# A second group of down chunks by Strassen's algorithm, one group amid gate and up, and a residual kept without ALPHA

## The chip, the cores and the metric

The kernel runs on one core of one Trainium2 chip. TensorE multiplies matrices, VectorE (DVE) and ScalarE (ACT) work element by element, GpSimd (POOL) and SyncE (SP) only issue transfers here. The metric is the device time of one execution in microseconds (us), from several runs, of which the median counts. Inputs lie in the chip's memory; the weights are reordered on the host before the launch, which is not timed.

## The reference

Two layers on x of 512 tokens by 1024 features, float32. Each layer is an FFN, a mixer (attention in layer 0, causal pooling in layer 1) and a second FFN, each with a residual and a layer norm, so there are six phases: FFN, attention, FFN, FFN, pooling, FFN.

```
def swiglu(x, w_gu, w_down):
    g, u = jnp.split(x @ w_gu, 2, axis=-1)        # w_gu: 1024 x 5632
    return (jax.nn.silu(g) * u) @ w_down          # w_down: 2816 x 1024

for i in range(DEPTH):                            # DEPTH = 2, ALPHA = 4 ** 0.25
    x = layer_norm(ALPHA * x + 0.5 * swiglu(x, ...), ln_g[i, 0], ln_b[i, 0])
    x = layer_norm(ALPHA * x + mixer(x), ln_g[i, 1], ln_b[i, 1])
    x = layer_norm(ALPHA * x + 0.5 * swiglu(x, ...), ln_g[i, 2], ln_b[i, 2])
```

layer_norm takes mean and variance over the 1024 features, adds 1e-5 to the variance, multiplies by g and adds b.

## The kernel before, in words

**Products.** Every float32 operand is split into a high part of reduced precision (ScalarE, L97) and the rest (VectorE, L98), and each product is three matmuls: high by low, high by high, low by high (mm3, L100 to L104). One split handles 128 partitions by 1024 elements.

**Weights.** They come as pieces of 128x1024 (512 KB). `load` (L181) issues a piece on SP into a slot of 4 KB per partition; a piece with `plus` gets a second block added by an accumulating transfer on the POOL queue (L187). `prepare` (L197) splits the next unit into a high and a low slot; raw pieces and split parts share 24 slots (SLOTS). `load_ahead` keeps up to 7 or 9 pieces loaded (RAW, and two more if `free()` allows), `run_ahead` keeps 5 parts and more prepared beyond those retired (PARTS, L208 to L212). `held` counts slots taken by other tiles.

**FFN.** The 22 chunks of 128 hidden features are handled in pairs. Pair 0 is plain; pairs 1 to 10 are quads: Strassen's algorithm with seven products (numbered 1 to 7) in place of eight, over two halves of the tokens, two halves of the input features, and gate with up. A unit of a quad is one product: two outputs, four k, three passes, 24 matmuls of 256 columns. ORDER (L150) lists the units; all x operands (seven tiles with tag "act", ACT = 7 buffers of 8 KB) live until the last quad. The result, silu(gate) times up, goes to hT for features 0 to 7 (BLOCK = 8) and to slots (`later`) for the rest.

**Down.** Features 0 to 7 go through Strassen's algorithm as well, after the last quad: seven products in the order LATER = (1, 2, 6, 5, 7, 3, 4), each with two weight tiles, two k, two token tiles and three passes, 24 matmuls of 512 columns, and each followed by two additions from PSUM into the residual ax on VectorE (L626). Their operands are made by a generator (`seven`, L295): a sum or difference where it takes one (`form`), then the split (`take`) into an "act" buffer; each `next(operands)` makes the next. The remaining 14 chunks are plain (BProduct, L418): main handles a chunk for four token tiles with 24 matmuls, and the last four chunks (five in the last phase) form a tail that goes token tile by token tile, so that the layer norm of one lies beside the matmuls of the next. Their operands are splits of pairs of chunks (`act`, L633).

**Residual.** ax holds the normalised rows of all tokens. During the phase after, VectorE turns each token tile into ALPHA times (row times g plus b), by two operations of 128x1024 (L392, L393), or one multiplication in the first FFN (L390). The rows of g and b are broadcast into tiles with tag "stage" (four buffers of 4 KB), which the feature-major copies of x use too.

**What sets the order.** TensorE runs in the order of the code. For the other engines and the queues a planner orders the instructions: at each moment of its own time model the earliest in the code among those that are ready; a tile that finds no free buffer waits for one. `tc.issue_after` puts an instruction behind another on its engine. The order is fixed at compile time, and each engine and queue then works in order. ORDER and two more places set where in the code an operand is made or a residual tile updated:

```
    ORDER = [(1, 1)] + [(i, jj + (i == 1)) for jj in QUADS for i in (2, 6, 5, 7, 3, 1, 4) if (i, jj) != (1, QUADS[-1])]
                    if 3 <= jj < 3 + NT:
                        update_residual(ins)
                if jj == QUADS[-1] and i in (2, 6, 3):
                    next(operands)
```

Of the kernel before, what the change touches and what calls it, by code (L numbers as in the profile page):

```python
# [32 lines left out]
P = 128  # L33
# [17 lines left out]
BLOCK = 8  # L51
R = 4
R_LAST = 5
SLOTS = 24
RAW = 7
PARTS = 5
ACT = 7
# [23 lines left out]
def trunk(ctx, tc, x, rel_bias, ln_g, ln_b, w_gu, w_dq, w_down, a_in, a_out, b_in, b_group, b_scale, b_out, onehot, out):  # L81
# [68 lines left out]
    ORDER = [(1, 1)] + [(i, jj + (i == 1)) for jj in QUADS for i in (2, 6, 5, 7, 3, 1, 4) if (i, jj) != (1, QUADS[-1])]  # L150

    def ffn_units(l, m):
        for i in range(4):
            plain(w_gu[l, m, 0, i])
        gu = {jj: Quad(w_gu[l, m, jj]) for jj in QUADS}
        for i, jj in ORDER:
            gu[jj].unit(i)
        both = [Quad(w_dq[l, m, q]) for q in range(2)]
        pieces[-10:] = [q.pieces[i] for group in ((0,), (1,), (2,), (3,), (4,)) for q in both for i in group]
        for i in LATER:  # L160
            for q in both:
                q.unit(i)
        b_plain(w_down[l, m], range(BLOCK, NF))

# [14 lines left out]
    parts, taken, retired, held = [], [0], [0], [0]  # L179
# [63 lines left out]
    class Plain:  # L243

        def __init__(self, name):
            self.name, self.st, self.parts = name, {}, {}

        def stage(self, half, h):
            if (half, h) not in self.st:
                self.st[half, h] = lnp.tile([P, 4, 256], F32, tag="stage", bufs=4, name=f"st{self.name}_{half}_{h}")  # L250
            return self.st[half, h]
# [14 lines left out]
    class Seven(Plain):  # L266
# [20 lines left out]
        def sums(self):  # L287

            b11, b21, b12, b22 = (self.st[i] for i in ((0, 0), (1, 0), (0, 1), (1, 1)))
# [5 lines left out]
        def seven(self, b11, b21, b12, b22, room):  # L295
# [7 lines left out]
            self.form(6, u2, b11, -1.0, b22, ALU.subtract)  # L303
            self.take(5, b11)
# [27 lines left out]

    def ln_params(n):
        l, i = lns[n]
        gt = lnp.tile([P, D], F32, tag="stage", bufs=4, name=f"lng{n}")
        bt = lnp.tile([P, D], F32, tag="stage", bufs=4, name=f"lnb{n}")
        nc.sync.dma_start(gt, ln_g[l, i:i + 1, :].to_broadcast([P, D]))
        nc.sync.dma_start(bt, ln_b[l, i:i + 1, :].to_broadcast([P, D]))
        return gt, bt

    class LayerNorm:
        def __init__(self, n, t, scale):
            self.n, self.t, self.scale = n, t, scale
# [8 lines left out]
        def normalize(self, gt, bt):  # L352
# [4 lines left out]
            nc.vector.tensor_scalar(ve, var, EPS, None, op0=ALU.add)  # L357
# [19 lines left out]
    row = [None, None]  # L377

    def load_residual():
        if residual[0][1] is not None:  # L380
            row[:] = ln_params(residual[0][1])
# [120 lines left out]
    def ffn(n, x, dest):  # L502
        with tc.tile_pool(name=f"ffn{n}", bufs=1) as fp:
            hT = fp.tile([P, BLOCK, S], F32, name=f"hT{n}")
            later, kept = {}, {}

            def features(f):

                return hT[:, f, :] if f < BLOCK else later[f // 2][:, f % 2, :]

            def room(jj):

                if 2 * jj >= BLOCK:
# [32 lines left out]
            for h, xi in enumerate(((1, 2), (8, 3))):  # L546
# [12 lines left out]
                if h == 0:  # L559
                    x.sums()  # L560

            hid = Seven(f"h{n}")
            hv = hT.rearrange("p (j c) s -> p j c s", c=2)
            operands = hid.seven(*(hv[:, 0:BLOCK // 2, c, h * 256:(h + 1) * 256] for h in range(2) for c in range(2)),
                                 lambda: fp.tile([P, 4, 256], F32, tag="ca", name=f"u2{n}"))

            quads = {}
            for i, jj in ORDER:
                if n == 0 and (i, jj) == (1, 2):
                    columns()  # L570
                    onehots = bias_load()
# [31 lines left out]
                if jj == QUADS[-1] and i in (2, 6, 3):  # L603
                    next(operands)

            accs = {0: (bank(0, f"da{n}_0"), bank(1, f"da{n}_1"))}
            for i in LATER:
                if i in (2, 5):  # L610
                    g = BANKS[i]
                    accs[g] = [bank(2 * g + t, f"d{n}_{i}_{t}") for t in range(2)]
                acc = accs[BANKS[i]]
                for q in range(2):
                    wh, wl = weights()
                    for k in range(2):
                        c = slice(k * 512, (k + 1) * 512)
                        for t in range(2):
                            o = hid.parts[i][:, :, 2 * q + k, t * P:(t + 1) * P]
                            mm3(acc[t], o[:, 0], o[:, 1], wh[:, c], wl[:, c], q == 0 and k == 0 and i in (1, 2, 5),  # L620
# [292 lines left out]
```

## Time and profile before

| | |
|---|---|
| median of 3 runs | 1727.77 us (1726.58 to 1728.12) |
| the profiled execution | 1726.37 us |
| its span, first to last instruction | 1724.2 us |
| granted TensorE clock over the span | 0.999 of full speed (2.4 GHz) |
| bytes moved by transfers | 257.30 MB, 149 GB/s on average |

The profile shows one execution. Busy time is the time in which an engine works on an instruction; matmuls overlap each other, so the time from one start to the next is shorter than one matmul's duration. PE is TensorE's matmuls, PEld its weight loads beside them. L98 is line 98 of the kernel. A wait is the idle time of an engine before an instruction, with what ended it.

### The profile page before, as it was taken

How to read it: one execution, taken by the hardware profiler on the slowest of the kernel's cores; microseconds unless marked ns; L12 is line 12 of the kernel's file. 1: busy time of each engine (PE TensorE's matmuls, PEld its weight loads, DVE VectorE, ACT ScalarE, POOL GpSimd, SP SyncE). 2: the span in 40 equal slices, each digit the busy share in tenths (PEclk: the TensorE clock that was granted, in tenths of full speed). 3: DMA queues.
4: the chain of work that ended last, by engine and by line, in shares of the span. 5: the costliest groups of instructions: out<-in, count | busy, mean ns of one | idle time of the engine just before them, and what ended most of it. 6: DMA issues, size and time to landing. Idle time of an engine off the chain costs nothing.

```text
span 1724.2 us, 27993 instructions
## 1 busy us (share of the span) xinstructions
PE 1701.4 (99%) x11555; PEld 1582.5 (92%) x11555; DVE 1240.8 (72%) x1657; ACT 824.8 (48%) x1161; POOL 93.8 (5%) x132
## 2 busy tenths in 40 slices
PE   8999999999999999999999999999999999999998
PEld 8999998898888899999888999998898899999886
DVE  6876697365666977778929777789279887777945
ACT  6544455164444554445525544455244464455620
POOL 1120000000000000000000000000000000000000
PEclk9999999999999999999999999999999999999999
DMA  9776566232224376655743766657322556665611
GB/s 306 194 233 176 141 175 218 78 99 86 85 81 129 77 203 172 172 149 142 238 123 76 204 173 170 149 144 235 98 74 98 145 173 176 171 172 153 183 51 49
DMA packets 84863, 257.30 MB, mean 149 GB/s; under 512 B 8128, under 2 KB 25576, under 8 KB 84736
## 3 DMA queue, kind: packets, MB, share of 16 engines
q1 hardware_dynamic: 70080, 202.40, 35.6%
q0 software_dynamic: 14656, 53.12, 17.9%
q8 instruction: 90, 1.47, 0.4%
q14 instruction: 37, 0.30, 0.1%
HBM read 253.37 MB, written 4.74 MB: 150 GB/s over the span
## 4 chain that ended last, share of the span: by engine, by line
PE 94%; DVE 4%; DMA 1%; issue 1%; ACT 0%; SPq 0%; DVEq 0%; POOLq 0%
PE gu L102 17%; PE gu L103 17%; PE gu L104 17%; PE acc L102 7%; PE acc L104 7%; PE acc L103 7%; PE qk L102 2%; PE qk L103 2%; PE qk L104 2%; PE da L102 2%; PE da L103 2%; PE da L104 2%; PE d L102 1%; PE d L103 1%; PE d L104 1%; DVE lo L98 1%
## 5 line engine op out<-in xcount | busy, mean ns | idle before, releaser
L102 PE MATMUL gu<-x,hi 128*128 128x256 f32 x2496 | 708.7, 284 | 5.3 <-DVE x L98 5.3
L98 DVE TENSOR_TENSOR lo<-raw,hi 128x1024 fp32r<-128x1024 f32 x458 | 555.8, 1221 | 211.3 <-PE acc L102 92.5
L103 PE MATMUL gu<-x,hi 128*128 128x256 f32 x2496 | 706.8, 283 | 0.0
L104 PE MATMUL gu<-x,lo 128*128 128x256 f32 x2496 | 706.8, 283 | 0.0
L97 ACT ACTIVATE hi<-raw 128x1024 fp32r<-128x1024 f32 x458 | 479.2, 1056 | 369.0 <-DVE lo L98 252.4
L102 PEld LDWEIGHTS gu<-x,hi 128*128 128x128 f32 x2496 | 479.7, 192 | 8.3 <-DVE x L98 7.1
L103 PEld LDWEIGHTS gu<-x,hi 128*128 128x128 f32 x2496 | 479.7, 192 | 0.0
L104 PEld LDWEIGHTS gu<-x,lo 128*128 128x128 f32 x2496 | 479.6, 192 | 0.0
L102 PE MATMUL acc<-lo,h 128*128 128x512 f32 x448 | 174.8, 390 | 0.0
L104 PE MATMUL acc<-hi,h 128*128 128x512 f32 x448 | 174.3, 389 | 0.0
L103 PE MATMUL acc<-hi,h 128*128 128x512 f32 x448 | 174.3, 389 | 0.0
L187 POOL DMA_DIRECT2D raw<-in_ffn_w_gu x80 | 68.7, 859 | 1061.6 <-DMA raw<-in_ffn_w_gu 606.9
L140 DVE TENSOR_TENSOR raw<-raw,raw 128x1024 f32<-128x1024 f32 x96 | 117.1, 1220 | 8.6 <-DMA raw<-in_ffn_w_dq 7.2
L522 ACT ACTIVATE kept<-gu 128x512 f32<-128x512 f32 x120 | 71.1, 592 | 98.5 <-PE gu L104 98.5
L104 PEld LDWEIGHTS acc<-hi,h 128*128 128x128 f32 x448 | 84.1, 188 | 17.6
L103 PEld LDWEIGHTS acc<-hi,h 128*128 128x128 f32 x448 | 84.1, 188 | 17.2
L102 PEld LDWEIGHTS acc<-lo,h 128*128 128x128 f32 x448 | 84.1, 188 | 17.1
L525 DVE TENSOR_TENSOR cb<-gu,kept 128x512 f32<-128x512 f32 x40 | 27.6, 689 | 67.7 <-PE gu L104 67.7
L349 DVE SCALAR_TENSOR_TENSOR ax<-acc,ax 128x512 f32<-128x512 f32 x48 | 33.0, 688 | 55.7 <-PE acc L104 55.3
L328 ACT ACTIVATE st<-tp,cols 128x128 f32<-128x128 f32 x140 | 53.5, 468 | 23.7 <-PE tp L317 23.7
L529 ACT ACTIVATE sg<-cb 128x256 f32<-128x256 f32 x40 | 16.5, 412 | 94.5 <-DVE cb L525 94.5
L98 DVE TENSOR_TENSOR x<-st,x 128x512 fp32r<-128x512 f32 (+1 forms) x64 | 51.4, 820 | 12.2 <-ACT x L97 12.2
(155 smaller groups left out, 2193.5 us busy)
## 6 DMA issues: line engine op xcount, KB each, us to landing
raw<-in_ffn_w_gu SPq DMA_DIRECT2D x216, 512.0 KB, 4.6
raw<-in_ffn_w_gu POOLq DMA_DIRECT2D x80, 512.0 KB, 6.3
raw<-in_ffn_w_down SPq DMA_DIRECT2D x56, 512.0 KB, 4.3
raw<-in_ffn_w_dq SPq DMA_DIRECT2D x40, 512.0 KB, 3.6
raw<-in_a_w_in SPq DMA_DIRECT2D x24, 512.0 KB, 3.9
raw<-in_ffn_w_dq POOLq DMA_DIRECT2D x16, 512.0 KB, 6.8
raw<-in_a_w_out SPq DMA_DIRECT2D x8, 512.0 KB, 3.6
raw<-in_b_w_in SPq DMA_DIRECT2D x8, 512.0 KB, 5.2
```

The lines of the kernel that those rows point to most:

```text
L97: nc.scalar.activation(hi, src, AF.Copy)
L98: return nc.vector.tensor_tensor(lo, src, hi.bitcast(F32), op=ALU.subtract)
L102: nc.tensor.matmul(acc, sh, ml, start=first, stop=False, skip_group_check=shared)
L103: nc.tensor.matmul(acc, sh, mh, start=False, stop=False, skip_group_check=shared)
L104: nc.tensor.matmul(acc, sl, mh, start=False, stop=last, skip_group_check=shared)
L140: nc.vector.tensor_tensor(d, d, more, op=ALU.add)
L187: nc.gpsimd.dma_start(p.tile, p.plus, accum_op=ALU.add)
L328: nc.scalar.activation(src[:, i, :], tp[:, c], AF.Identity, scale=g, bias=b)
L349: nc.vector.scalar_tensor_tensor(r, y, self.scale, r, op0=ALU.mult, op1=ALU.add)
L522: nc.scalar.activation(kept[i, jj], acc, AF.Copy)
L525: nc.vector.tensor_tensor(out, two(acc), two(kept.pop((i, jj))), op=ALU.add)
L529: nc.scalar.activation(sg, g, AF.Silu, scale=sign)
```

## The change

Sixteen of the 22 down chunks go through Strassen's algorithm, in two groups of eight. The products of the first group stand in ORDER at quad 7 (MIDDLE): the first of them before that quad's unit 4, the other six behind it. Those of the second group follow the last quad. Six chunks stay plain. There are nine "act" buffers and 20 slots; the four "stage" buffers become one of 16 KB, which holds the second group's features too, and the norms' rows go to slots. The operand of a product is made after the weights of later ones in the code (`retire`, then `next(operands)`), and in the first group one call each at units 6 and 7 of quad 7 and after products 1, 2, 6, 5 and 7. ax is kept without ALPHA: its sums are divided by ALPHA and the norm's epsilon by ALPHA squared. Its g is multiplied in by one VectorE operation, its b added by an accumulating broadcast transfer on the POOL queue; the first FFN's rows need neither. Pooling's pT goes to "act" buffers.

```diff
-SLOTS = 24
+SLOTS = 20
+GROUP = 8
-BLOCK = 8
+BLOCK = 16
-ACT = 7
+ACT = 9
+MIDDLE = 7
...
+    ORDER = [(1, 1)]
+    for jj in QUADS:
+        after = [] if jj == QUADS[-1] else [(1, jj + 1)]
+        seven = [(i, jj) for i in (2, 6, 5, 7, 3, 4)]
+        if jj == MIDDLE:
+            group = [(i, FF) for i in LATER]
+            ORDER += seven[:-1] + group[:1] + seven[-1:] + group[1:] + after
+        else:
+            ORDER += seven[:-1] + after + seven[-1:]
+    ORDER += [(i, FF + g) for g in range(1, BLOCK // GROUP) for i in LATER]
...
     def free():
-        return SLOTS - RAW - 2 * PARTS - held[0]
+        return SLOTS - RAW - 2 * PARTS - sum(held)
 
     def load_ahead():
-        while len(loaded) < len(pieces) and sum(p.uses > 0 for p in loaded[-32:]) < RAW + 2 * (free() > 1):
+        while len(loaded) < len(pieces) and sum(p.uses > 0 for p in loaded[-32:]) < RAW + 2 * (free() > 1) + min(0, free()):
             load()
...
             self.form(6, u2, b11, -1.0, b22, ALU.subtract)
+            yield
             self.take(5, b11)
...
     def update_residual(after, count=1):
 
-        with tc.issue_after(after.ins):
-            for _ in range(count):
-                t, n = residual.pop(0)
-                gt, bt = row
-                if n is None:
-                    nc.vector.tensor_scalar(ax[:, t, :], ax[:, t, :], ALPHA, None, op0=ALU.mult)
-                else:
-                    nc.vector.scalar_tensor_tensor(ax[:, t, :], ax[:, t, :], ALPHA, gt, op0=ALU.mult, op1=ALU.mult)
-                    nc.vector.scalar_tensor_tensor(ax[:, t, :], bt, ALPHA, ax[:, t, :], op0=ALU.mult, op1=ALU.add)
+        for _ in range(min(count, len(residual))):
+            t, n = residual.pop(0)
+            with tc.issue_after(after.ins):
+                nc.vector.tensor_tensor(ax[:, t, :], ax[:, t, :], row[0], op=ALU.mult)
+            nc.gpsimd.dma_start(ax[:, t, :], ln_row(ln_b, n), accum_op=ALU.add)
+            if not residual:
+                held[1] = 0
...
+            hid = [Seven(f"h{n}_{g}") for g in range(BLOCK // GROUP)]
+
+            def form():
+
+                for g, h in enumerate(hid):
+                    hv = hT[g].rearrange("p (j c) s -> p j c s", c=2)
+                    yield from h.seven(*(hv[:, :, c, t * 256:(t + 1) * 256] for t in range(2) for c in range(2)),
+                                       lambda: fp.tile([P, 4, 256], F32, tag="ca", name=f"u2{n}_{g}"))
+
+            operands = form()
+            accs = {}
+
+            def down_product(i, g):
+
+
+                if i in (1, 2, 5):
+                    b0 = {1: (2, 6), 2: (0, 2), 5: (4, 4)}[i][g]
+                    accs[g, BANKS[i]] = [bank(b0 + t, f"d{n}_{g}_{i}_{t}") for t in range(2)]
+                acc = accs[g, BANKS[i]]
+                for q in range(2):
+                    wh, wl = weights()
+                    for k in range(2):
+                        c = slice(k * 512, (k + 1) * 512)
+                        for t in range(2):
+                            o = hid[g].parts[i][:, :, 2 * q + k, t * P:(t + 1) * P]
+                            mm3(acc[t], o[:, 0], o[:, 1], wh[:, c], wl[:, c], q == 0 and k == 0 and i in (1, 2, 5),
+                                q == 1 and k == 1 and i in (2, 3, 4), True)
+                for t0, d, sign in {1: ((0, 0, 1),), 2: ((0, 0, 1),), 6: ((2, 0, 1),), 5: ((2, 1, -1),), 7: ((2, 1, -1),),
+                                    3: ((2, 0, 1),), 4: ((0, 1, -1),)}[i]:
+                    for t in range(2):
+                        r = ax[:, t0 + t, d * 512:(d + 1) * 512]
+                        nc.vector.scalar_tensor_tensor(r, acc[t], 0.5 / ALPHA * sign, r, op0=ALU.mult, op1=ALU.add)
+                retire(2)
+                if i in ((1, 2, 6, 5, 7) if g == 0 else (1, 2, 6, 5)):
+                    next(operands)
...
-                if jj == QUADS[-1] and i in (2, 6, 3):
+                if (i, jj) in ((6, MIDDLE), (7, MIDDLE), (2, QUADS[-1]), (6, QUADS[-1]), (3, QUADS[-1])):
                     next(operands)
...
-            down.main((3, 1, 2, 0))
+            down.main((1, 0, 2, 3))
...
     def pooling(n, x, dest):
-        held[0] = 6
+        held[0] = 0
...
-                    pT[g] = [wp.tile([P, 2, S], F32R, tag="slot", bufs=SLOTS, name=f"pT{i}_{g}") for i in range(2)]
+                    pT[g] = glob.tile([P, 2, 2, S], F32R, tag="act", bufs=ACT, name=f"pT{g}")
```

## Rows read from the trace of the kernel before

**Rows 1.** The page: busy time by engine, and the chain that ended last.

```profile
...
PE 1701.4 (99%) x11555; PEld 1582.5 (92%) x11555; DVE 1240.8 (72%) x1657; ACT 824.8 (48%) x1161; POOL 93.8 (5%) x132
...
PE 94%; DVE 4%; DMA 1%; issue 1%; ACT 0%; SPq 0%; DVEq 0%; POOLq 0%
...
```

**Rows 2.** Who made TensorE wait (us in total, times, longest).

```profile
...
PE gu L102 <- DVE x L98: 5.3, 6, 1.0
...
```

**Rows 3.** Busy time by stage: seven down products, plain down, a quad.

```profile
...
core 0: us, PE busy (x) PEld busy (x) DVE busy (x) ACT busy (x) POOL busy (x), PEclk, DMA share, GB/s
239.30:277.40 38.10, 38.10 (x171) 31.54 (x170) 38.10 (x42) 26.70 (x28) 1.20 (x3) 1.00 0.70 218
277.40:331.90 54.50, 54.50 (x242) 45.16 (x241) 21.26 (x20) 13.68 (x13) 0.00 (x0) 1.00 0.44 137
1440.30:1460.50 20.20, 20.20 (x170) 20.20 (x170) 13.89 (x16) 10.29 (x14) 1.71 (x2) 1.00 0.71 183
...
```

**Rows 4.** Groups by line and shape: busy us, mean ns | idle before.

```profile
...
L98 DVE TENSOR_TENSOR lo<-raw,hi 128x1024 fp32r<-128x1024 f32 x458 | 555.8, 1221 | 211.3 <-PE acc L102 92.5 <-ACT hi L97 71.6 <-PE gu L103 27.0
...
L97 ACT ACTIVATE hi<-raw 128x1024 fp32r<-128x1024 f32 x458 | 479.2, 1056 | 369.0 <-DVE lo L98 252.4 <-PE gu L103 50.1 <-issue 28.4
...
L140 DVE TENSOR_TENSOR raw<-raw,raw 128x1024 f32<-128x1024 f32 x96 | 117.1, 1220 | 8.6 <-DMA raw<-in_ffn_w_dq 7.2
...
L102 PE MATMUL da<-lo,xh 128*128 128x512 f32 x128 | 49.8, 389 | 0.0
...
L393 DVE SCALAR_TENSOR_TENSOR ax<-lnb,ax 128x1024 f32<-128x1024 f32 x20 | 24.1, 1219 | 0.0
...
L626 DVE SCALAR_TENSOR_TENSOR ax<-da,ax 128x512 f32<-128x512 f32 x32 | 20.5, 684 | 0.0
...
L187 POOL DMA_DIRECT2D raw<-in_ffn_w_dq x16 | 13.7, 854 | 170.4 <-DMA raw<-in_ffn_w_dq 72.0 <-DVE lo L98 67.3 <-DVE hT L530 22.8
...
```

**Rows 5.** TensorE in order of time: start us, duration, instruction.

```profile
...
236.30 0.39 PE L102 MATMUL gu<-x,hi 128*128 128x256 f32 x1
...
239.28 0.40 PE L102 MATMUL da<-lo,xh 128*128 128x512 f32 x1
...
252.91 0.39 PE L102 MATMUL da<-lo,xh 128*128 128x512 f32 x1
...
255.63 0.39 PE L102 MATMUL d<-lo,xh 128*128 128x512 f32 x1
...
```

**Rows 6.** VectorE in order of time, about those starts.

```profile
...
238.82 0.68 DVE L525 TENSOR_TENSOR ca<-gu,kept 128x512 f32<-128x512 f32 x1
...
252.90 1.28 DVE L626 SCALAR_TENSOR_TENSOR ax<-d,ax 128x512 f32<-128x512 f32 x2
254.10 1.22 DVE L98 TENSOR_TENSOR xh<-hT,xh 128x1024 fp32r<-128x1024 f32 x1
255.23 2.35 DVE L98 TENSOR_TENSOR lo<-raw,hi 128x1024 fp32r<-128x1024 f32 x2
257.50 1.28 DVE L626 SCALAR_TENSOR_TENSOR ax<-da,ax 128x512 f32<-128x512 f32 x2
...
```

**Rows 7.** VectorE in order of time, before and in the first FFN's tail.

```profile
...
331.59 1.23 DVE L98 TENSOR_TENSOR lo<-raw,hi 128x1024 fp32r<-128x1024 f32 x1 [4.22 <-PE acc L102]
...
353.52 1.22 DVE L98 TENSOR_TENSOR lo<-raw,hi 128x1024 fp32r<-128x1024 f32 x1
...
356.77 1.23 DVE L98 TENSOR_TENSOR lo<-raw,hi 128x1024 fp32r<-128x1024 f32 x1
...
```

**Rows 8.** TensorE in order of time, where attention starts.

```profile
...
356.31 0.39 PE L102 MATMUL qk<-x,hi 128*128 128x256 f32 x1 [0.80 <-DVE x L98]
...
```

**Rows 9.** DMA issues: KB each, median us to landing.

```profile
...
raw<-in_ffn_w_dq SPq DMA_DIRECT2D x40, 512.0 KB, 3.6
...
raw<-in_ffn_w_dq POOLq DMA_DIRECT2D x16, 512.0 KB, 6.8
...
```

**Rows 10.** Who made VectorE wait for weight transfers.

```profile
...
DVE raw L140 <- DMA raw<-in_ffn_w_dq: 7.2, 6, 2.0
...
```

More of the change, by code (lines that the diff above doesn't have):

```diff
@@ L154, in ffn_units @@
             plain(w_gu[l, m, 0, i])
-        gu = {jj: Quad(w_gu[l, m, jj]) for jj in QUADS}
+        made = {}
         for i, jj in ORDER:
[L157 to L162, printed above, removed]
+            if jj < FF:
+                if i == 1:
+                    made[jj] = Quad(w_gu[l, m, jj])
+                made[jj].unit(i)
+            else:
+                if i == 1:
+                    both = [Quad(w_dq[l, m, 2 * (jj - FF) + q]) for q in range(2)]
+                    pieces[-10:] = [q.pieces[k] for k in range(5) for q in both]
+                for q in both:
+                    q.unit(i)
         b_plain(w_down[l, m], range(BLOCK, NF))
@@ L177, in trunk @@
     ffn_units(1, 1)
-    parts, taken, retired, held = [], [0], [0], [0]
+    parts, taken, retired, held = [], [0], [0], [0, 0]
     def load():
@@ L245, in __init__ @@
         def __init__(self, name):
-            self.name, self.st, self.parts = name, {}, {}
+            self.name, self.st, self.parts = name, None, {}
         def stage(self, half, h):
-            if (half, h) not in self.st:
-                self.st[half, h] = lnp.tile([P, 4, 256], F32, tag="stage", bufs=4, name=f"st{self.name}_{half}_{h}")
-            return self.st[half, h]
+            if self.st is None:
+                self.st = lnp.tile([P, 4, 4, 256], F32, tag="stage", name=f"st{self.name}")
+            return self.st[:, 2 * half + h]
         def parts_of(self, half):
@@ L287, in sums @@
         def sums(self):
-            b11, b21, b12, b22 = (self.st[i] for i in ((0, 0), (1, 0), (0, 1), (1, 1)))
+            b11, b21, b12, b22 = (self.stage(*i) for i in ((0, 0), (1, 0), (0, 1), (1, 1)))
             self.form(5, b11, b11, 1.0, b12, ALU.subtract)
@@ L329, in to_feature_major, with ln_row @@
         dest.put(t, half, src)
+    def ln_row(w, n):
+        l, i = lns[n]
+        return w[l, i:i + 1, :].to_broadcast([P, D])
     def ln_params(n):
[L334 to L339, printed above, removed]
+        rows = []
+        for nm, w in (("g", ln_g), ("b", ln_b)):
+            rows.append(wp.tile([P, D], F32, tag="slot", bufs=SLOTS, name=f"ln{nm}{n}"))
+            nc.sync.dma_start(rows[-1], ln_row(w, n))
+        return rows
     class LayerNorm:
         def __init__(self, n, t, scale):
-            self.n, self.t, self.scale = n, t, scale
+            self.n, self.t, self.scale = n, t, scale / ALPHA
             self.st = lnp.tile([P, 12], F32, tag="st", bufs=2, name=f"st{n}_{t}")
@@ L560, in ffn @@
                     x.sums()
[L562 to L565, printed above, removed]
+            hid = [Seven(f"h{n}_{g}") for g in range(BLOCK // GROUP)]
[27 more added lines that the diff above has]
+                    next(operands)
             quads = {}
             for i, jj in ORDER:
+                if jj >= FF:
+                    down_product(i, jj - FF)
+                    continue
                 if n == 0 and (i, jj) == (1, 2):
@@ L872, in trunk @@
     late.append(lambda: [to_feature_major(xs[0], 3, half, ax[:, 3, :]) for half in range(2)] + [run_ahead()])
-    residual.extend((t, None) for t in range(NT))
     for i, phase in enumerate((ffn, attention, ffn, ffn, pooling, ffn)):
```

48 lines of the change are left out of this document (15 added, 33 removed).

## The prediction

> **What bounds the kernel now.** I read the page's shares and chain first, then who makes TensorE wait, then the stages by time. TensorE is busy for 1701.4 of 1724.2 us, and the chain that ends last lies on it for 94% [rows 1]. It waits almost for nothing: the largest wait inside the work is 5.3 us in six pieces, at the starts of phases, for a layer-normed input [rows 2]. So time is TensorE's own work, and a matmul less is time less, as long as VectorE keeps its operands coming. That is the second thing to see: in the 38.1 us of the seven down products VectorE is busy for all 38.1 us, in a quad of gate and up for 13.89 of 20.20, in the plain down stage for 21.26 of 54.50 [rows 3]. VectorE is full in one stage only, and the change doubles that stage.
>
> **What goes from TensorE.** Eight plain chunks are 8 x 4 x 2 x 3 = 192 matmuls of 128x512; by seven products of two weight tiles, two k, two t and three passes they are 168. 24 go per FFN, 96 in all. A matmul's busy time of 389 ns [rows 4] is not its price, since they overlap; the pitch is. From 252.91 to 255.63 twelve start, 0.2267 us each [rows 5], and the whole stage says the same: 38.10/168 = 0.2268 [rows 3]. 96 x 0.2267 = **21.8 us**.
> The Trainium skill (TensorE: Matmul & The Clock Gate, Back-to-back issue gap) gives about 131 ns as the sustained spacing of 512-column matmuls. By it the 96 would be worth an estimated 12.6 us. The trace's stage of the same matmuls disagrees, with 226.7 ns, and the measurement decides.
>
> **What comes to VectorE and ScalarE.** Per FFN: 14 weight splits in place of 8 (+6), 4 weight sums, 7 operand splits in place of 4 pairs (+3), 4 operand sums, and 14 additions into ax. A 128x1024 operation takes 1.22 us alone and 1.135 us in a row, a pair of additions 1.20 us (250.63, 252.90, 254.10) [rows 4, 6]. That is 17 x 1.135 + 14 x 0.60 = 27.7 us per FFN, 111 us in all. The second residual operation goes: 20 x 1.14 = 23 us [rows 4] (the first FFN's four multiplies go too, uncounted). VectorE ends near 1240.8 + 111 - 23 = 1329 us of some 1705, ScalarE gains 9 x 1.06 x 4 = 38 us on 825 [rows 1, 4]. Neither becomes the bound over the whole; the question is local.
>
> **The middle group (products amid quad 7).** Its VectorE work is 29 operations x 1.135 + 14 x 0.60 = 41.3 us, beside 38.1 us of products and 2.88 us of the one gate/up unit among them (24 x 0.12 us, 236.30 to 239.28 with the next start [rows 5]). So it is as full as the stage before was, and that one starved nothing, because its operands were split far ahead. Here they can't be: the quad's x still holds seven of nine operand buffers, so two remain, and the operand of a product can be split only when the product two before it has ended. Behind that end VectorE has, in the order that the code issues: the two additions (1.20), one weight split whose slots come free at the same moment (1.14; the other's come half a product earlier), then the operand's split (1.22, ScalarE's 1.06 beside the first two). Before, additions began late: TensorE left a product at 255.63, the addition began at 257.50, 1.87 us on, for VectorE was in two weight splits [rows 5, 6]. 1.87 + 1.20 + 1.14 + 1.22 = 5.43 us against the 5.44 us of the product between. Nothing is left over, and nothing much is lost. Bounds: zero, if VectorE comes to the additions at once (3.6 of 5.44 us; the quads before leave it 6.3 us free each [rows 3], in which sums can go ahead); 4.5 us per FFN, if both weight splits stand in front (6.56, 1.12 too much, for the four operands of products 5, 7, 3 and 4). I take 1.0 us per FFN, nearer to the zero end, as a late operand gives VectorE the same time to catch up: **+4.0 us**. Product 6 has the gate/up unit as extra cover.
>
> **The group at the end.** Seven products as before, x's buffers coming free under them, fewer plain splits beside them. One thing is new: the first product writes bank 6, which the last quad's unit 3 used. That unit ended at 236.30, VectorE read its bank from 238.82 to 239.50, and the first product would start at 239.28 [rows 5, 6]. 0.2 us late, with a semaphore 0.3; bounds 0 and 1.2 us (one split more in front of it). 4 x 0.3 = **+1.2 us**. Behind it two plain chunks and four tail ones (six instead of fourteen, 32.6 us) hold three pairs of operand splits instead of seven; VectorE has 33 us idle there now [rows 3], so this cover may shrink.
>
> **Twenty slots instead of 24.** Working parts and raw pieces claim them all, before as after: the last split before the tail waited 4.22 us for TensorE to give a slot back [rows 7]. In the tail four parts are held to its end. Before, the tail's planning went six parts past the retired chunks, now five, so that one or two parts fewer of the next phase lie ready. The next ones were split at 353.52 and 356.77 [rows 7]. An FFN asks for its second part 2.88 us after its start, its third 5.76: covered. Attention and pooling ask for the third part 1.44 us after theirs, 356.31 + 1.44 = 357.75 [rows 8], and one place later it is ready at 356.77 + 1.23 = 358.0. I take 0.5 us for each of those two, **+1.0 us**, bounds 0 and 3.2 us (the spacing of the two splits).
>
> **At nothing.** Loads: six more 512 KB transfers per FFN, about 12.6 MB on 257, in stages that move 140 to 220 GB/s [rows 3]; a piece lands 3.6 us after its issue, an accumulated one 6.8 [rows 9], and nine pieces (in the last group seven) are loaded ahead. The bias transfers: twenty accumulations on the POOL queue, 0.85 us of issue each, with POOL busy 1.71 us of a quad [rows 3, 4]; behind each waits the next weight accumulation of that queue, and behind that VectorE's weight sum, which waited 7.2 us in six times for such transfers without TensorE noticing [rows 2, 10]. If that cover is gone a transfer costs up to 6.8 us; I take 0, since the pieces are loaded several units ahead. The bias lands a quad or more before ax is next read. The normalisation's constants change no instruction; its rows now come through slots, on SP, with nothing urgent behind them. The order of tiles in the plain stage follows the banks that come free; 4.1 us separate the last product from its banks' reuse, as before.
>
> **Sum.** The profiled execution took 1726.37 us (span 1724.2 and 2.2 around it), 1.4 under the median 1727.77. 1726.4 - 21.8 + 4.0 + 1.2 + 1.0 = 1710.8; on the median's footing **1712 us**.
>
> **Rivals.**
> - The operand waits eat the gain. Weight splits are issued ahead of the operand, so both may stand before it: 1.12 us for each of four operands, 17.9 us in all, 1727.8 - 21.8 + 17.9 + 2.2 = 1726, no change. For it: the order of the code, and the lag of 1.87 us. Against: half a product of earlier slots for one of the splits.
> - Slower: the same queue with the operand's own sum in it. The place is the middle group, products 7 and 4, whose operand needs a sum, then ScalarE's copy, then the split. If none of it is done ahead: 1.87 + 1.20 + 2.27 + 1.14 + 1.06 + 1.22 = 8.8 us against 5.44, 3.3 us each, with 1.12 for products 5 and 3: 8.9 us per FFN, 1727.8 - 21.8 + 35.6 + 2.2 = 1744. It decides from 1.2 us per operand on (19.6 us over sixteen). For it: VectorE full for 41 us. Against: the sums read features that are ready since quad 3, and the quads before have room for them.
> - Each removed matmul is worth less than its pitch. The nearest row for a lower price is the 256-column matmul's 0.12 us [rows 5]: 96 x 0.12 = 11.5 us, less 6.2 of waits, so 1722. For it: weight loads take 1582.5 us of TensorE's span beside the matmuls [rows 1]. Against: the whole stage runs at 0.2268. The Trainium skill's spacing, named above, would put it near this rival.
>
> **Chances.** The forecast 0.68, its own range 1705 to 1719. No change by operand waits 0.15 (a third of it still faster). Slower by the sums 0.11. Cheaper matmuls 0.06. A measurement of this kernel tells 0.2%, 3.5 us, from no change. Faster 0.68 + 0.06 + 0.05 = 0.79; same 0.08; slower the rest, 0.13. The lower end is the full 21.8 us with no wait (1706) and a run's spread; the upper end, 1727, takes in the cheap matmuls and the eaten gain, and leaves the slower case out.
>
> **What would show it.** TensorE with 96 matmuls of 128x512 fewer and the same pitch of 0.227 us in both groups; its waits for VectorE's operand copies (xh) near 1 us per FFN, all in the middle group; VectorE near 1329 us. Gaps of more than 1.2 us before products 5, 7, 3 and 4 would be the slower rival, waits on the bank at the first product of the last group the small one, a wait for weight parts at the starts of attention and pooling the slots. It is wrong if TensorE's idle time grows by more than 10 us, or if it starves at a place not named here.

## The result, and the profile after

The median fell from 1727.17 us (six runs, 1726.13 to 1728.12) to **1713.65 us** (six runs, 1711.82 to 1715.64), a ratio of 0.9922 with a 95% interval of 0.9909 to 0.9934: 13.5 us faster, where 15.8 were forecast. The profiled execution took 1713.76 us, its span is 1712.0 us, 12.2 less than before. So it came out as forecast in sign and size, but two errors of opposite sign stand in the working: the size is in part luck, and one of the errors is the lesson of this case.

The page, busy time by engine and the chain that ended last, as [rows 1]:

```profile
...
PE 1684.5 (98%) x11459; PEld 1564.8 (91%) x11459; DVE 1328.1 (78%) x1757; ACT 860.1 (50%) x1197; POOL 125.7 (7%) x168
...
PE 87%; DVE 7%; DMA 4%; issue 1%; ACT 1%; SPq 0%; DVEq 0%; POOLq 0%; ACTq 0%
...
```

VectorE has 1328.1 us, as worked out (1329), ScalarE 860.1 (863). The 96 matmuls are gone (11555 to 11459). But TensorE's share of the chain fell from 94% to 87%, and DMA has 4% of it now. Who made TensorE wait (us in total, times, longest), as [rows 2]:

```profile
...
PE d L104 <- ACT xh L99: 4.0, 3, 2.1
PE gu L104 <- DVE x L100: 3.4, 6, 0.8
PE d L106 <- DVE xh L100: 2.3, 3, 0.8
...
```

There is a new wait, 6.3 us for operands of the down products (xh), in three places of two pieces each. The old wait for x has shrunk from 5.3 to 3.4 us. A wait is not all that is lost: taking each start of a matmul less the one before, and from that the undisturbed pitch (0.2267 us for 512 columns, 0.12 for 256), the sum over the whole trace, transposes left out, is 15.4 us before and 25.2 us after, so 9.8 of the 21.8 us came back as loss. I call this sum lost time below. It lies in the middle groups of three FFNs: 0.04 us in the first, 4.8, 3.0 and 2.4 in the others, 10.1 in these three. Such a figure comes from the one execution that was profiled. In this trace and in those of five versions below that leave these three groups alike, or try a cure that does not work, one group lost 2.2 to 5.0 us and the three 9.1 to 12.1 in all; a difference of a microsecond or two between such runs shows no effect. The windows of these four groups, in order (busy time of each engine, clock, DMA share, GB/s), as [rows 3]:

```profile
...
core 0: us, PE busy (x) PEld busy (x) DVE busy (x) ACT busy (x) POOL busy (x), PEclk, DMA share, GB/s
175.60:216.60 41.00, 41.00 (x194) 34.42 (x193) 39.07 (x43) 22.23 (x23) 3.45 (x4) 1.00 0.74 199
738.90:784.70 45.80, 42.93 (x195) 35.29 (x194) 43.67 (x47) 24.00 (x26) 3.46 (x4) 0.96 0.77 194
1082.40:1126.30 43.90, 41.82 (x194) 34.16 (x193) 41.69 (x46) 23.33 (x25) 3.45 (x4) 1.00 0.76 199
1528.40:1571.80 43.40, 42.00 (x195) 34.28 (x194) 41.18 (x45) 23.31 (x25) 3.45 (x4) 1.00 0.79 204
...
```

The first FFN's group has no idle TensorE in 41.0 us. The second's lasts 45.8. What the first FFN lacks, beside everything that they share, is a residual with g and b: no row is loaded, nothing multiplied, no bias transferred.

Inside the second one. TensorE, in order of time (start, duration), as [rows 5]:

```profile
...
755.00 0.50 PE L104 MATMUL d<-lo,xh 128*128 128x512 f32 x1 [2.09 <-ACT xh L99]
...
756.50 0.79 PE L106 MATMUL d<-hi,xh 128*128 128x512 f32 x1 [0.77 <-DVE xh L100]
757.10 0.63 PE L104 MATMUL d<-lo,xh 128*128 128x512 f32 x1
757.52 0.63 PE L105 MATMUL d<-hi,xh 128*128 128x512 f32 x1
...
```

The matmul at 755.00 is the first of product 6, and it waited 2.09 us for ScalarE's part of its operand and then 0.77 for VectorE's. VectorE, as [rows 6]:

```profile
...
732.19 1.23 DVE L142 TENSOR_TENSOR raw<-raw,raw 128x1024 f32<-128x1024 f32 x1 [2.79 <-DMA raw<-in_ffn_w_dq]
...
738.79 1.22 DVE L142 TENSOR_TENSOR raw<-raw,raw 128x1024 f32<-128x1024 f32 x1 [4.24 <-DMA raw<-in_ffn_w_dq]
...
752.55 1.22 DVE L300 SCALAR_TENSOR_TENSOR u<-hT 128x1024 f32<-128x1024 f32 x1
...
755.23 1.22 DVE L100 TENSOR_TENSOR xh<-u,xh 128x1024 fp32r<-128x1024 f32 x1
...
```

It stood at two weight sums (L142) for 2.79 and 4.24 us, because the pieces that they add had not landed. It works in order, so everything planned behind them came later by that: 13.8 us after the start of the second of them the difference for operand 6 (u), and behind that its split (755.23). By TensorE's time product 6 was due at 752.7. And the POOL queue, where those pieces are accumulated:

```profile
...
722.59 0.86 POOL L203 DMA_DIRECT2D raw<-in_ffn_w_dq  x1 [18.63 <-DMA raw<-in_ffn_w_dq]
723.26 1.08 POOL L412 DMA_DIRECT2D ax<-in_ln_b  x1
725.46 0.86 POOL L203 DMA_DIRECT2D raw<-in_ffn_w_dq  x1 [1.11 <-ACT sg L552]
...
```

Between the weight accumulations of 722.59 and 725.46 stands the bias transfer of quad 6. The issues of that stretch (716 to 745 us; KB, median us to landing), as [rows 9]:

```profile
...
raw<-in_ffn_w_dq SPq DMA_DIRECT2D x6, 512.0 KB, 6.0
raw<-in_ffn_w_dq POOLq DMA_DIRECT2D x4, 512.0 KB, 9.5
ax<-in_ln_b POOLq DMA_DIRECT2D x1, 512.0 KB, 12.7
...
```

The weight accumulations took 9.5 us there, the bias transfer 12.7. Over the whole run VectorE's sums waited 31.6 us for such pieces, 18.5 of it at the first two sums for these three groups; 7.2 before [rows 10]:

```profile
...
L104 PE MATMUL d<-lo,xh 128*128 128x512 f32 x448 | 175.8, 392 | 4.4 <-ACT xh L99 4.0
...
L142 DVE TENSOR_TENSOR raw<-raw,raw 128x1024 f32<-128x1024 f32 x112 | 136.8, 1221 | 33.4 <-DMA raw<-in_ffn_w_dq 31.6
...
```

### The profile page after: what moved, and what is told of

The parts are those of the page before. It is cut to its first block, busy times and chain, and to the rows that moved or that the text cites. A ratio compares the mean times of both kernels' runs of the same rounds, so it can differ in the third digit from the quotient of the medians.

```text
span 1712.0 us, 28171 instructions
## 1 busy us (share of the span) xinstructions
PE 1684.5 (98%) x11459; PEld 1564.8 (91%) x11459; DVE 1328.1 (78%) x1757; ACT 860.1 (50%) x1197; POOL 125.7 (7%) x168
## 2 busy tenths in 40 slices
DMA packets 90482, 277.77 MB, mean 162 GB/s; under 512 B 8752, under 2 KB 26200, under 8 KB 90352
## 4 chain that ended last, share of the span: by engine, by line
PE 87%; DVE 7%; DMA 4%; issue 1%; ACT 1%; SPq 0%; DVEq 0%; POOLq 0%; ACTq 0%
PE gu L104 16%; PE gu L106 15%; PE gu L105 15%; PE d L106 5%; PE d L104 5%; PE d L105 5%; PE acc L106 4%; PE acc L105 4%; PE acc L104 4%; DMA raw<-in_ffn_w_dq 4%; DVE lo L100 2%; PE qk L104 2%; PE qk L106 2%; PE qk L105 2%; PE tp L334 1%
## 5 line engine op out<-in xcount | busy, mean ns | idle before, releaser
L99 ACT ACTIVATE hi<-raw 128x1024 fp32r<-128x1024 f32 x482 | 505.8, 1058 | 449.2 <-DVE lo L100 182.5
L100 DVE TENSOR_TENSOR lo<-raw,hi 128x1024 fp32r<-128x1024 f32 x482 | 585.1, 1219 | 154.4 <-ACT hi L99 133.9
L104 PE MATMUL d<-lo,xh 128*128 128x512 f32 x448 | 175.8, 392 | 4.4 <-ACT xh L99 4.0
L106 PE MATMUL d<-hi,xh 128*128 128x512 f32 x448 | 175.6, 392 | 2.3 <-DVE xh L100 2.3
L105 PE MATMUL d<-hi,xh 128*128 128x512 f32 x448 | 175.0, 391 | 0.0
L142 DVE TENSOR_TENSOR raw<-raw,raw 128x1024 f32<-128x1024 f32 x112 | 136.8, 1221 | 33.4 <-DMA raw<-in_ffn_w_dq 31.6
L104 PEld LDWEIGHTS d<-lo,xh 128*128 128x128 f32 x448 | 84.5, 189 | 23.1 <-ACT xh L99 5.3
L106 PEld LDWEIGHTS d<-hi,xh 128*128 128x128 f32 x448 | 84.5, 189 | 22.1 <-DVE xh L100 4.5
L105 PEld LDWEIGHTS d<-hi,xh 128*128 128x128 f32 x448 | 84.5, 189 | 17.1
L545 ACT ACTIVATE kept<-gu 128x512 f32<-128x512 f32 x120 | 70.5, 587 | 55.6 <-PE gu L106 55.4
L104 PE MATMUL acc<-lo,h 128*128 128x512 f32 x192 | 75.3, 392 | 0.0
L106 PE MATMUL acc<-hi,h 128*128 128x512 f32 x192 | 74.8, 389 | 0.0
L105 PE MATMUL acc<-hi,h 128*128 128x512 f32 x192 | 74.8, 389 | 0.0
L616 DVE SCALAR_TENSOR_TENSOR ax<-d,ax 128x512 f32<-128x512 f32 x112 | 72.4, 681 | 1.6 <-PE d L106 1.5
```

The lines of the kernel that those rows point to most:

```text
L99: nc.scalar.activation(hi, src, AF.Copy)
L100: return nc.vector.tensor_tensor(lo, src, hi.bitcast(F32), op=ALU.subtract)
L104: nc.tensor.matmul(acc, sh, ml, start=first, stop=False, skip_group_check=shared)
L105: nc.tensor.matmul(acc, sh, mh, start=False, stop=False, skip_group_check=shared)
L106: nc.tensor.matmul(acc, sl, mh, start=False, stop=last, skip_group_check=shared)
L142: nc.vector.tensor_tensor(d, d, more, op=ALU.add)
```

## The experiments

**Theory T**, formed on these rows: a bias transfer that stands in the POOL queue ahead of a weight accumulation of the middle group makes it land late; VectorE, in order, stands at the weight sum; the difference for operand 6, planned behind it, is late, and TensorE waits. **Rival A**, the forecast's own: VectorE is too full, with two operand buffers and the weights ahead of the operand. **Rival B**: the slot that the g row holds until quad 6 makes the group's loads late. What an experiment does to the middle groups is given as lost time of the four FFNs, after the change 0.04, 4.8, 3.0, 2.4.

**No bias transfer.**

```diff
                 nc.vector.tensor_tensor(ax[:, t, :], ax[:, t, :], row[0], op=ALU.mult)
-            nc.gpsimd.dma_start(ax[:, t, :], ln_row(ln_b, n), accum_op=ALU.add)
```

> Leaves out the twenty accumulating transfers of the bias row (so b is missing from the residual); VectorE's multiplication by g and the slot of the g row stay. Theory T (the transfer behind quad 6 stands in the POOL queue and on the DMA rings between the weight accumulations of the middle group, VectorE stands in order at a weight sum until they land, and the difference for operand 6 comes late): the waits of TensorE in the middle groups, 10.1 us over three FFNs, fall to under 2 us, 1704 to 1706 us. Rival A (VectorE is simply too full with two operand buffers): VectorE has the same work, the waits stay at 8 us or more, 1712 to 1714. Rival B (the slot that the g row holds until quad 6 makes the loads of the group late): the waits stay for the most part, 6 to 10 us.

1706.0 us (ratio to the kernel before 0.9879, 0.9864 to 0.9894), lost time 0.04, 0.5, 0.05, 0.7. T holds, A falls: VectorE does the same work and TensorE hardly waits. The same stretch of the second FFN, POOL and its landings, then VectorE:

```profile
...
722.60 0.86 POOL L203 DMA_DIRECT2D raw<-in_ffn_w_dq  x1 [24.40 <-DMA raw<-in_ffn_w_dq]
725.46 0.86 POOL L203 DMA_DIRECT2D raw<-in_ffn_w_dq  x1 [2.00 <-DMA raw<-in_ffn_w_dq]
...
```

```profile
...
raw<-in_ffn_w_dq SPq DMA_DIRECT2D x6, 512.0 KB, 4.8
raw<-in_ffn_w_dq POOLq DMA_DIRECT2D x4, 512.0 KB, 7.9
...
```

```profile
...
731.52 1.23 DVE L142 TENSOR_TENSOR raw<-raw,raw 128x1024 f32<-128x1024 f32 x1 [1.99 <-DMA raw<-in_ffn_w_dq]
...
735.59 1.22 DVE L142 TENSOR_TENSOR raw<-raw,raw 128x1024 f32<-128x1024 f32 x1 [1.71 <-DMA raw<-in_ffn_w_dq]
...
749.35 1.22 DVE L300 SCALAR_TENSOR_TENSOR u<-hT 128x1024 f32<-128x1024 f32 x1
...
```

The second accumulation was issued at the same moment, 725.46, but the sum that needs it began at 735.59, not 738.79. So the bias transfer costs no time on the issuing queue; it costs 3.2 us on the way. The Trainium skill (DMA: Bandwidth & Descriptors, Issuing engines are not separate DMA queues) says that transfers from all engines share the same 16 DMA engines, and that more issuing engines save no more than issue time. The pair of runs agrees with the first half: beside the bias transfer the pieces issued on SP land later too, in a median of 6.0 us, not 4.8. No run here issues the bias transfer from another engine. The 3.2 us are no accident of this FFN: in the traces of the changed kernel and all its versions below, the second accumulation of a middle group took 11.6 to 13.3 us to land where a bias transfer stands just ahead of it (19 places) and 7.8 to 10.0 where none does.

**The update a quad earlier.**

```diff
-                    if 3 <= jj < 3 + NT:
+                    if 2 <= jj < 2 + NT:
```

> The residual's update of an FFN behind quads 2 to 5 instead of 3 to 6: same work, a quad further from the middle group, and the slot of the g row free a quad earlier. T and rival B alike: waits in the middle groups under 2 us, 1704 to 1706 us, a version faster than both. Rival A: quad 6 gives VectorE 1.1 us more room, no more: the waits stay at 7 us or more, 1711 to 1713.

1704.85 us (0.9873, 0.9856 to 0.9889); lost time 0.04 us in each of the four groups. With one number changed 8.8 us come back (8.4 when each version is held against the kernel before in its own runs). Its POOL queue, the landing in the same window (716 to 745 us), and VectorE:

```profile
...
720.08 0.86 POOL L203 DMA_DIRECT2D raw<-in_ffn_w_dq  x1 [16.26 <-DMA raw<-in_ffn_w_dq]
722.85 0.86 POOL L203 DMA_DIRECT2D raw<-in_ffn_w_dq  x1 [1.91 <-DMA raw<-in_ffn_w_dq]
...
```

```profile
...
raw<-in_ffn_w_dq POOLq DMA_DIRECT2D x4, 512.0 KB, 6.4
...
```

```profile
...
729.29 1.21 DVE L142 TENSOR_TENSOR raw<-raw,raw 128x1024 f32<-128x1024 f32 x1
...
731.68 1.22 DVE L142 TENSOR_TENSOR raw<-raw,raw 128x1024 f32<-128x1024 f32 x1
...
746.32 1.22 DVE L300 SCALAR_TENSOR_TENSOR u<-hT 128x1024 f32<-128x1024 f32 x1
...
749.01 1.22 DVE L100 TENSOR_TENSOR xh<-u,xh 128x1024 fp32r<-128x1024 f32 x1
...
```

The second accumulation is issued 2.6 us earlier than in the two runs above (722.85), and the accumulations land in a median of 6.4 us; VectorE waits for neither sum, and the difference is made at 746.32, 6.2 us earlier than after the change: 3.2 us are the transfer's (752.55 to 749.35 in the run without it), 3.0 the earlier issue's. The earlier issue goes with the g row's slot, which is free a quad sooner: wherever that slot is held until quad 6 the second accumulation is issued 12.8 to 13.6 us ahead of the group, with or without transfers, and wherever it is not, 14.2 to 15.9, also in the first FFN of the run below that multiplies at quad 6 there and holds no row. Rival B is thus part of it: in the run without transfers, which holds the slot, 1.1 us more is lost over the three FFNs (0.5 and 0.7 us in two of them), here nothing.

**The operand ahead of the weights in the code.**

```diff
-                retire(2)
                 if i in ((1, 2, 6, 5, 7) if g == 0 else (1, 2, 6, 5)):
                     next(operands)
+                retire(2)
```

> In the down products the next operand is made ahead of the next weights in the code, not behind them. T: what is late is the difference for operand 6 behind the weight sums, so putting it ahead takes some of the wait away, 2 to 6 us of the 10.1, but VectorE still stands at a weight sum for 3 to 4 us in three FFNs. Rival A: the order of two weight splits and an operand was the cause, the waits fall to under 1 us, about 1704.

1713.61 us in one run; lost time 0.04, 2.2, 2.9, 4.2: 9.4 in all against 10.2, no more than such runs differ by. Rival A's cure does not cure, and T's estimate of some relief missed too. In the second FFN the difference does come sooner behind the late sum, 12.6 us instead of 13.8, but a sum for a later operand now stands ahead of its split, which comes 16.0 us behind the late sum instead of 16.4.

**Transfers added to the first FFN.**

```diff
                         update_residual(ins)
+                        if n == 0:
+                            nc.gpsimd.dma_start(ax[:, jj - 3, :], ln_row(ln_b, 0), accum_op=ALU.add)
```

> Adds four accumulating transfers of a bias row to the first FFN too, behind quads 3 to 6 (its residual is then wrong by those rows); no VectorE work and no g row is added there. That FFN has no wait in its middle group now (0.04 us). T: it gets one of 1.5 to 5 us, as the others have, 1715 to 1718 us. Rivals A and B: it stays under 0.5 us, 1713 to 1714.

1716.21 us, but not for the reason expected: the first FFN's middle group lost 0.04 us. With nothing on VectorE to hold them back the transfers were issued at the start of the phase (9.3 to 21.5 us), far from quads 3 to 6, and TensorE lost 2.2 us at 41 us, in a wait that the trace puts down to ScalarE's copy of a unit's result (L545); what made that late was not followed up. A test of a place has to make sure of the place.

**Only quad 6's transfer left out.**

```diff
...
-            nc.gpsimd.dma_start(ax[:, t, :], ln_row(ln_b, n), accum_op=ALU.add)
+            if bias:
+                nc.gpsimd.dma_start(ax[:, t, :], ln_row(ln_b, n), accum_op=ALU.add)
...
-                        update_residual(ins)
+                        update_residual(ins, bias=jj < 6)
```

> Leaves out only the bias transfer behind quad 6 in each FFN (four of twenty; b is then missing from one token tile); those behind quads 3 to 5 stay. T: this one alone stands among the weight accumulations of the middle group, so the waits of TensorE there fall from 10.1 us to what the run without any transfer has left, 1 to 2 us, 1705 to 1707 us. If transfers load the DMA rings over a longer stretch, the waits stay at 4 us or more.

1705.83 us in one run, lost time 0.04, 0.4, 0.6, 0.4: what the run without any transfer has. Twenty transfers are five phases of four, and the first FFN has none, so three stand at quad 6 of an FFN (the expectation counted four). The other seventeen cost nothing that these runs show; without the three beside the group's accumulations 8.8 of the 10.1 us are gone.

**The bias on VectorE.**

```diff
...
-            row[0] = wp.tile([P, D], F32, tag="slot", bufs=SLOTS, name=f"lng{n}")
-            nc.sync.dma_start(row[0], ln_row(ln_g, n))
-            held[1] = 1
+            row[:] = ln_params(residual[0][1])
+            held[1] = 2
...
                 nc.vector.tensor_tensor(ax[:, t, :], ax[:, t, :], row[0], op=ALU.mult)
-            nc.gpsimd.dma_start(ax[:, t, :], ln_row(ln_b, n), accum_op=ALU.add)
+                nc.vector.tensor_tensor(ax[:, t, :], ax[:, t, :], row[1], op=ALU.add)
...
-                    if 3 <= jj < 3 + NT:
+                    if 2 <= jj < 2 + NT:
```

> The bias added by VectorE from a second row slot, no bias transfers, updates behind quads 2 to 5: 1.14 us more of VectorE in each of twenty places, 23 us in all, and one slot less while the rows are held. T: no transfer stands in the way, VectorE has 6 us free in these quads, so within 2 us of the version with transfers a quad earlier, 1704 to 1707. Rival A (VectorE too full): 3 us slower or more, 1708 and up.

1705.31 us (0.9873, 0.9856 to 0.9889), lost time 0.04 in each group. 21 us more of VectorE by the profiles' pages (1349.5, against 1328.8 in the run with the update a quad earlier) change nothing: A falls a second time, and the bias by transfers gains nothing over the old way of adding it, once it stands where it does no harm.

**The first FFN again, gated.** Its tiles are multiplied by 1 on VectorE behind unit 3 of quads 3 to 6, with and without the transfer behind that:

```diff
                         update_residual(ins)
+                        if n == 0:
+                            with tc.issue_after(ins.ins):
+                                nc.vector.tensor_scalar(ax[:, jj - 3, :], ax[:, jj - 3, :], 1.0, None, op0=ALU.mult)
+                            nc.gpsimd.dma_start(ax[:, jj - 3, :], ln_row(ln_b, 0), accum_op=ALU.add)
```

> In the first FFN each token tile is multiplied by 1 on VectorE behind quads 3 to 6, and a bias row is added to it by a transfer behind that (its residual is then wrong by that row). The multiplication keeps the transfer in its place, which the run before lacked: there the transfers were issued at the phase's start. T: the first FFN's middle group gets a wait of 0.5 to 5 us (it holds no row slot, which made up some 2.6 us of the lateness elsewhere), 1714 to 1719 us.

> The same multiplications by 1 in the first FFN without the transfers. T: no wait in its middle group, under 0.2 us, 1713 to 1714 us. If VectorE's 0.69 us per quad are the cause, the same wait as with the transfers.

1713.72 us with, 1716.16 us without; lost time of the first FFN's group 0.04 us in both, so T's number missed (of the 2.4 us between the two, 2.2 is lost time in the middle groups of later FFNs, which are coded alike). The POOL queue of the run with the transfer says why:

```profile
...
157.31 0.86 POOL L203 DMA_DIRECT2D raw<-in_ffn_w_dq  x1 [15.37 <-DMA raw<-in_ffn_w_dq]
160.53 0.86 POOL L203 DMA_DIRECT2D raw<-in_ffn_w_dq  x1 [2.37 <-DVE ax L656]
161.07 1.21 POOL L657 DMA_DIRECT2D ax<-in_ln_b  x1
...
```

Here the bias transfer (161.07) stands behind the second weight accumulation (160.53), not ahead of it as in the later FFNs, and that sum waited 0.24 us. T needs the order, not the neighbourhood. So the same once more, a unit earlier:

```diff
-                    gate(2 * jj + 1, 256, 512, cb[:, 0, :], cb[:, 1, :], -1.0)
+                    ins = gate(2 * jj + 1, 256, 512, cb[:, 0, :], cb[:, 1, :], -1.0)
+                    if n == 0 and 3 <= jj < 3 + NT:
+                        with tc.issue_after(ins.ins):
+                            nc.vector.tensor_scalar(ax[:, jj - 3, :], ax[:, jj - 3, :], 1.0, None, op0=ALU.mult)
+                        nc.gpsimd.dma_start(ax[:, jj - 3, :], ln_row(ln_b, 0), accum_op=ALU.add)
```

> As the gated transfer in the first FFN, but a unit earlier (behind unit 7 of quads 3 to 6), so that it stands in the POOL queue ahead of the second weight accumulation of the middle group, as in the later FFNs, and not behind it. T: that accumulation then lands 3 us later, VectorE stands at its sum for 2 to 4 us, and the first FFN gets a wait of TensorE of 0.3 to 2 us in its middle group (its loads come 2.6 us earlier than elsewhere, for want of a row slot). If a transfer in the queue does not matter, no wait: under 0.1 us.

1714.97 us in one run. Its POOL queue, and VectorE at the sum and the split of operand 6; behind them the same two of VectorE in the run with the multiplications alone:

```profile
...
157.83 0.86 POOL L203 DMA_DIRECT2D raw<-in_ffn_w_dq  x1 [19.05 <-DVE ax L659]
159.02 0.86 POOL L660 DMA_DIRECT2D ax<-in_ln_b  x1 [0.33 <-issue]
160.93 0.86 POOL L203 DMA_DIRECT2D raw<-in_ffn_w_dq  x1 [1.05 <-ACT kept L545]
...
```

```profile
...
173.29 1.23 DVE L142 TENSOR_TENSOR raw<-raw,raw 128x1024 f32<-128x1024 f32 x1 [3.98 <-DMA raw<-in_ffn_w_dq]
...
189.74 1.22 DVE L100 TENSOR_TENSOR xh<-u,xh 128x1024 fp32r<-128x1024 f32 x1
...
```

```profile
...
169.35 1.23 DVE L142 TENSOR_TENSOR raw<-raw,raw 128x1024 f32<-128x1024 f32 x1 [0.58 <-DMA raw<-in_ffn_w_dq]
...
185.93 1.22 DVE L100 TENSOR_TENSOR xh<-u,xh 128x1024 fp32r<-128x1024 f32 x1
...
```

Now the transfer (159.02) is ahead of the second accumulation (160.93). The sum that needs it waited 3.98 us (0.58 in the run with the multiplications alone), operand 6 was split at 189.74 to 190.96 instead of 185.93 (the whole group lies 0.9 us later in this run), and TensorE, due at 190.4, lost 0.6 us in a group that had lost none. Moving one transfer by one place in a queue made the wait. That it is 0.6 us and not 3 goes with the first FFN's head start, the rest of rival B: the accumulation is issued 15.7 us ahead of the group, 13.3 to 13.6 in the later FFNs. So neither cause makes the loss alone. The held slot by itself costs 0.4 us per FFN (1.2 over three), the transfer by itself 0.6 in this one place, both together 3.4.

The same run shows the pattern once more: behind the bias transfer of quad 3 stands a transfer for attention's position bias (gd), VectorE waited 3.84 us for it at 102 us (0.59 after the change), and TensorE lost 1.4 us at 109 to 113.

**The residual's part alone, on the kernel before.** ax without ALPHA, g by VectorE, b by transfers; the Strassen part, slots and buffers as before:

```diff
...
-                    nc.vector.scalar_tensor_tensor(ax[:, t, :], ax[:, t, :], ALPHA, gt, op0=ALU.mult, op1=ALU.mult)
-                    nc.vector.scalar_tensor_tensor(ax[:, t, :], bt, ALPHA, ax[:, t, :], op0=ALU.mult, op1=ALU.add)
...
+                nc.vector.tensor_tensor(ax[:, t, :], ax[:, t, :], row[0], op=ALU.mult)
+            nc.gpsimd.dma_start(ax[:, t, :], ln_b[l, i:i + 1, :].to_broadcast([P, D]), accum_op=ALU.add)
```

> The kernel before with the residual's part of the change alone: ax without ALPHA, g by VectorE, b by twenty bias transfers behind quads 3 to 6 and in attention and pooling; eight Strassen chunks, 24 slots and seven operand buffers stay. T: the transfers do harm only beside weight accumulations that something waits for soon; in this kernel the down group's come after quad 8, so there is no wait, and VectorE's 23 us less lie under TensorE: within 1.5 us of the kernel before, 1725.5 to 1728.5. If the transfers as such cost TensorE time, 1730 and more.

1725.66 us, ratio 0.9993 (0.9985 to 1.0002): no change. VectorE's sums waited 6.7 us for pieces, as before (7.2). The part is worth nothing by itself; what the change gains is the second group.

**Earlier update, and the old banks in the last group.**

```diff
-                    b0 = {1: (2, 6), 2: (0, 2), 5: (4, 4)}[i][g]
+                    b0 = {1: (2, 0), 2: (0, 2), 5: (4, 4)}[i][g]
...
-                    if 3 <= jj < 3 + NT:
+                    if 2 <= jj < 2 + NT:
...
-            down.main((1, 0, 2, 3))
+            down.main((3, 1, 2, 0))
```

> Updates behind quads 2 to 5, and the last group's first product on banks 2t of token tile 0 (0 and 1) with the plain tiles in the order 3, 1, 2, 0, as the kernel before had it: bank 6, which the last quad's unit 3 has just left, is not waited for. The forecast's term: three waits of 0.28 us go, 0.8 to 1.2 us, which a timing can't tell; in the trace the gap before the last group is under 0.1 us in all four FFNs. 1703.5 to 1705 us.

1702.66 us (0.9860, 0.9845 to 0.9875), the fastest of all, 11 us under the changed kernel and 24 under the one before. It is a little under its expectation. TensorE at the start of the last FFN's last group, in the changed kernel and in this one:

```profile
...
1632.28 0.28 PE L106 MATMUL gu<-x,lo 128*128 128x256 f32 x1
1632.69 0.50 PE L104 MATMUL d<-lo,xh 128*128 128x512 f32 x1
...
```

```profile
...
1621.63 0.28 PE L106 MATMUL gu<-x,lo 128*128 128x256 f32 x1
1621.75 0.40 PE L104 MATMUL d<-lo,xh 128*128 128x512 f32 x1
...
```

From the last matmul of the quad to the first of the group 0.41 us pass after the change, 0.12 here, the plain pitch. The bank's wait of 0.29 us is real, is there in three of four FFNs, and is gone. Of the 2.2 us between this run and the one with the earlier update alone, 1.1 is lost time (16.2 to 15.1); the rest these runs don't assign, and the two intervals overlap.

## Why the prediction was right, point by point

- *96 matmuls at 0.2267 us, 21.8 us.* Right. Where nothing waits, the spacing is 0.2267 us in both groups, and the version with the earlier update, with 16.2 us of lost time against 15.4 before, is 21.9 us faster than the kernel before in its own runs (1726.76 to 1704.85). The rival of cheap matmuls does not fit that, nor do the 131 ns of the Trainium skill (TensorE: Matmul & The Clock Gate, Back-to-back issue gap).
- *VectorE near 1329 us, not the bound.* Right, 1328.1; and 21 us more did no harm.
- *The middle group, +4.0 us.* The step that failed. It cost 10.1 us, and not by what I had named. Products 5, 7, 3 and 4, whose operands wait for a buffer, lost at most 0.2 us; product 6, which I took to have the extra cover of a gate/up unit, waited in three FFNs. Without the bias transfer beside it the term is 1.2 us, with the whole update a quad earlier 0.1. So the rivals built on the order of weights and operand (1726 and 1744) had no ground either.
- *The bias transfers, at nothing.* The cause of that failure. I wrote that behind each waits the next weight accumulation, and behind that VectorE's sum, and that a transfer costs up to 6.8 us if the cover is gone; then I took 0, "since the pieces are loaded several units ahead". The 7.2 us that VectorE had waited for such pieces before [rows 10] came in the very stage that the change moved to where the transfers are issued. The cover was spent, and an in-order VectorE handed the lateness on. Seventeen of the twenty cost nothing that the runs show; the three at quad 6 cost 8.8 of the 10.1 us, though for the most part only together with the slot that the g row holds, which I had also put at nothing. And I had counted the transfers' issue, not their bytes: each moves 512 KB, as much as a weight piece, and the bytes grew by 20.5 MB (257.30 to 277.77), not by 12.6.
- *The bank, +1.2 us.* Right in mechanism and size for one place: 0.28 us (0.3 foreseen), in three of four FFNs, 0.85 in all, and removed by another bank.
- *The starts of attention and pooling, +1.0 us.* Wrong, but small: both wait 0.80 us as before, for x, and no weight part was late. Fewer slots cost nothing there. The slots' price is elsewhere, in the row that holds one until quad 6 (about 1 us by itself).
- *Not foreseen:* some 14 us into three FFNs TensorE loses 0.62 us less each (0.95 to 0.33 us of wait for x), 1.9 us in all. The residual's part alone does not do it (1.11 us lost there in that run, as before; 0.49 after the change); which other part does was not tried.

The sum as it came: -21.8 + 10.1 + 0.85 - 1.9 + 0.5 that no row assigns = -12.2 us, the span's difference. The forecast of +6.2 against +9.6 of losses was near because the unforeseen gain and the overpriced starts stand against the underpriced group: that nearness is luck. Of the prediction's own signs of being wrong, 10 us more of idle TensorE was nearly reached (9.8 us of lost time), and starving at a place not named is true of product 6, which it had called covered.

## What to carry to other kernels

When work with transfers of its own is moved, list what else is in those queues at the new place, in order: a transfer that nobody waits for is not free if one that somebody waits for soon stands behind it. Where an engine works in order, a late piece costs the consumer of whatever is planned next, so look for the wait one step behind the place that is late. Two delays that each nearly fit into the cover can cost far more together than one by one: 0.4 and 0.6 us per FFN alone, 3.4 together. And the moved work may come back to its price by moving the other thing: one quad earlier for an update was worth more than 8 us.

## What the runs showed of the hardware that was not expected

After the pauses of 2.09 and 0.77 us in the second FFN's middle group the granted clock fell. Two windows behind them (columns as above):

```profile
...
756.00:759.00 3.00, 2.50 (x6) 2.02 (x7) 3.00 (x4) 1.45 (x3) 0.86 (x1) 0.50 0.98 156
759.00:762.00 3.00, 3.00 (x14) 2.44 (x13) 3.00 (x4) 1.69 (x2) 0.00 (x0) 0.94 1.03 203
...
```

From 756 to 759 us it is 0.50, the 1.2 GHz level, and the matmuls there start every 0.42 us, not 0.2267 (757.10 and 757.52 above); in the next window it is 0.94. That makes 1.6 of this group's 4.8 us. The other two groups, with pauses of 1.30 and 0.78 us and of 0.62 and 0.78 us, show 1.00 throughout. The length of the pauses does not settle it: in the run with the multiplications alone the clock fell behind 1.49 and 0.78 us (0.52 from 1546 to 1549 us), and in the run with the transfer ahead it stayed at 1.00 behind 1.73 and 0.78 us. Such a fall, about 1.5 us each time, is part of why groups coded alike differ from run to run.

And the accumulating transfers of 512 KB between 716 and 745 us took a median of 9.5 us to land with the bias transfer among them, 7.9 without it, the first two issued at the same times, and 6.4 in the run with the earlier update.
